# DeltaNet's output norm in two halves: the inner tokens inside the scan's last step, the outer ones behind it

## The chip, the cores and the metric

The kernel runs on one core of a Trainium2 chip. Its engines are TensorE (PE, with the weight loads shown apart as PEld), VectorE (DVE), ScalarE (ACT), GpSimd (POOL) and SyncE (SP, which issues most DMAs). The metric is the device time of one execution in microseconds. The kernel before takes 1773.67 us, the median of 3 runs (1772.34 to 1774.33).

## The reference, cut to what matters

One layer of a diffusion backbone works on 256 latent tokens and 256 context tokens, with 2048 channels. The combined input projection feeds latent attention and a bidirectional gated DeltaNet with 8 heads of 128 channels. The DeltaNet scans go over chunks of 64 tokens, one scan in each direction, the latent scans starting from the final context states; the outputs of both directions are added. What the change touches is the norm of that sum:

```
def dn_output(o, z, o_norm, dtype):
    y = rmsnorm(o.transpose(0, 2, 1, 3), o_norm) * silu(z)
    return y.reshape(b, t, h * dv)

merged = sigmoid(gate_mla) * (y_mla @ w_o_mla) + sigmoid(gate_dn) * (y_dn @ w_o_dn)
```

For each token and head, `o` is divided by the root mean square over its 128 channels, multiplied by a weight for each channel and by silu(z). Behind it stand the branch projections, the output projection, and a gated MLP with a convolution.

## The kernel before

Channels lie on the 128 partitions and tokens along the free dimension, so `o` is a tile of 128 partitions x 8 heads x 256 tokens, and `z` likewise. Every large product is made of a high and a low part of the float32 numbers: `split` writes the high part with ScalarE (L121) and the rest with VectorE (L122); `mm_hl` multiplies the high part of the weights with both parts of the activations (512 columns) and the low part of the weights with the high part alone (256 columns). Weights come over SP's queue in pieces of 512 KB and are split on the fly into six buffers of each part (NH = 6), each 512 columns wide.

A tile framework puts the other engines' instructions in an order by its own plan. TensorE's is written out by hand where `pe.pinned` is set, as it is during the scan and the norm. There a generator yields after each piece of scan work a number of nanoseconds, and a `Side` object fills that much time with other work: `fill` is the rest of the gate projections for the DeltaNet branch (16 tiles, four steps each, of which eight steps are done before) and the attention branch's projection with w_o_mla (16 tiles of two steps). A step is four pairs of products, counts as 1300, and `Side` makes steps while it owes time, so 56 + 32 = 88 steps in all. `ada` is the adaLN modulation, products on VectorE, with the share ADS = 0.3 of the time.

The scan has eight steps: the four chunks of the context, then the four latent ones; both directions are done at once, so at latent step `st` the forward scan writes chunk `st` and the backward scan chunk 3 - `st`. After the third latent step the tokens 64 to 191 (chunks 1 and 2) are complete; the last one adds to chunks 0 and 3. A step makes the products `kp` with the state, the subtraction `r` on VectorE, then yields CA = 4000; the products `yp`, copied to `y` by ScalarE, then CB = 3000; then the outputs `op`, the state's update `sp_` (not in the last step), the addition of `op` to `o` (L1355), and CC = 7000.

`o_norm` follows. It loads z's gate (`zo`) from memory, squares `o` by head on ScalarE (L1366, two buffers), sums the squares over the partitions with `col_sum` (four narrow products for each 128 tokens, against a column of ones), scales the sums (L1370), takes them to the power -0.5 on GpSimd in four quarters (`rsq`, L173), and multiplies `o` by `zo` head by head (L1374). After 5000 ns of fill it spreads each quarter of the factors over the partitions: `row_bcast` writes two diagonal matrices (the high and the low part, L179 to L185) and multiplies each with a matrix of ones, into `bp` (named obp in the profile); then `o` is multiplied by it (L1380) and split into `YD`, head by head, with ON = 3000 ns of fill for each quarter.

Then the pinned order ends, and the DeltaNet branch is projected: 16 tiles of w_o_dn, each eight pairs of products with `YD` (`brp<-YD` in the profile), then the output projection (`ops`).

`z` itself is made 440 us earlier, as the first eight tiles of another `fill`: `gate_fin` adds the two halves of the product, `z_fin` makes z (tanh(z/2) + 1) and multiplies by half of the norm's weight on ScalarE (L920); a DMA of ScalarE's queue stores it to `Zs`.

Of the kernel before, what the change touches and what calls it, by code (L numbers as in the profile page):

```python
# [8 lines left out]
F32 = mybir.dt.float32  # L9
F32R = mybir.dt.float32r  # L10
# [6 lines left out]
P = 128  # L17
D = 2048
KD = D // P
T = 256  # L20
# [11 lines left out]
AD = 0.55  # L32
GD0 = 2
SC = 7500
ON = 3000
CA = 4000
CB = 3000
CC = 7000
# [15 lines left out]
def hybrid_block(ctx: ExitStack, tc: tile.TileContext, io, dbg=None):  # L54
# [99 lines left out]
    def mm_hl(ps, M, w, x, first, last):  # L154

        hi, lo = w
        xf = x.rearrange("p a b -> p (a b)")
        if last and not first:
            pe.matmul(ps[:M, :T], lo, x[:, 0, :], start=False, stop=False)
            pe.matmul(ps[:M, :], hi, xf, start=False, stop=True)  # L160
        else:
            pe.matmul(ps[:M, :], hi, xf, start=first, stop=False)
            pe.matmul(ps[:M, :T], lo, x[:, 0, :], start=False, stop=last)
# [723 lines left out]
    Gs = dram.tile([2, P, KD, T], F32, name="Gs")  # L887
    pz = ctx.enter_context(pool_("pz", 3))

    def gate_fin(ps, out, fin):  # L890
        kept = isinstance(out, int)
        x = gk[:, out] if kept else pz.tile([P, T], F32, tag="zx", name="zx")
        gather(ps, P, x)
        if fin is None:
            act.activation(x, x, AF.Tanh, scale=0.5)
        else:
            fin(x)
        if not kept:
            act.dma_start(out, x)

    def gate_tiles(jobs):

        for w, f, out, fin in jobs:
            W = lazy_w(io[w][f])
            ps = psm.tile([P, 512], F32, tag="mm", name="gtp")
            for k in range(KD):
                mm_hl(ps, P, W(k * P), H[0][:, k], k == 0, k == KD - 1)
                if k % 4 == 3 and k < KD - 1:
                    yield 1300
            gate_fin(ps, out, fin)  # L910
            yield 1300
# [4 lines left out]
    def z_fin(x):  # L916
        t = pz.tile([P, T], F32, tag="zx", name="zt")
        act.activation(t, x, AF.Tanh, scale=0.5)
        dve.scalar_tensor_tensor(out=x, in0=t, scalar=1.0, in1=x, op0=ALU.add, op1=ALU.mult)
        act.activation(x, x, AF.Copy, scale=onh)  # L920

    fill = Side(gate_tiles([("wz", f, Zs[:, f], z_fin) for f in range(HEADS)] + [("wgm", f, Gs[0, :, f], None) for f in range(KD)]))
    pC = ctx.enter_context(ExitStack())
# [321 lines left out]
    def scan():  # L1245
# [11 lines left out]
        def load_kv(n):  # L1257
            kt, v = (jit[:, 2 * j + n % 2].rearrange("p (h c) -> p h c", c=P) for j in (0, 2))
            sync.dma_start(kt, KTs[steps[n]])
            sync.dma_start(v, Vs[steps[n]])  # L1260
            return kt, v
# [24 lines left out]
        for n, st in enumerate(steps):  # L1286
            kt, v = kv
            lat, first, last = st < 4, n == 0, n == 7
            if lat:
                qe = load_out(st)  # L1290
            if n and not last:
                ke = load_ke(n)
            if first:
                rs = [v[:, 4 * q : 4 * q + 4] for q in range(2)]
            else:
                rs = [ps1.tile([P, 4, P], F32, tag="r", name="r", bufs=2) for _ in range(2)]
                kps = [psa.tile([P, 4, P], F32, tag="aux", name="kp") for _ in range(2)]

                for h in range(HEADS):
                    for d in range(2):  # L1300
                        hs = slice(64 * d, 64 * d + 64)
                        pe.matmul(kps[h // 4][hs, h % 4], kt[:, h, hs], S[:, h, d ^ h % 2], start=True, stop=True)
                for h in range(HEADS):
                    dve.scalar_tensor_tensor(out=rs[h // 4][:, h % 4], in0=kps[h // 4][:, h % 4], scalar=negc[:, st, h : h + 1], in1=v[:, h], op0=ALU.mult, op1=ALU.add)
            if not last:
                kv = load_kv(n + 1)
            yield CA
            y = ps1.tile([P, 2, 4, P], F32, tag="y", name="y")
            yp = [psa.tile([P, 4, P], F32, tag="aux", name="yp") for _ in range(2)]
            for h in range(HEADS):  # L1310
                for d in range(2):
                    pe.matmul(yp[d][half_[d ^ h % 2], h // 2], tt[half_[d], h], rs[h // 4][half_[d], h % 4], start=True, stop=True)
            for d in range(2):
                act.copy(y[:, d], yp[d])
            if not last:
                tt = load_system(n + 1)
            yield CB
            if lat:
                op = [psm.tile([P, HEADS, 64], F32, tag="mm", name="op") for _ in range(2)]
                for h in range(HEADS):  # L1320
                    for m in half_:
                        for d in range(2):
                            r = d ^ h % 2
                            pe.matmul(op[r][m, h], y[half_[r], d, h // 2, m], av[half_[r], h], start=h == 0, stop=False)
                for h in range(HEADS):
                    for r in range(2):
                        for m in half_:
                            pe.matmul(op[r][m, h], S[:, h, r, m], qe[:, h, half_[r ^ h % 2]], start=False, stop=h == HEADS - 1)
            if not last and not first:
                for h in range(HEADS):  # L1330
                    for r in range(2):
                        act.activation(S[:, h, r], S[:, h, r], AF.Copy, scale=gend[:, r ^ h % 2, st, h : h + 1])
            if not last:
                for q in range(2):
                    h4 = slice(4 * q, 4 * q + 4)
                    sp = [psa.tile([P, 4, P], F32, tag="aux", name="sp_") for _ in range(2)]
                    for j in range(4):
                        h = 4 * q + j
                        for r in range(2):
                            pe.matmul(sp[r][:, j], ke[half_[r], h], y[half_[r], r ^ h % 2, h // 2], start=True, stop=True)  # L1340
                    for r in range(2):
                        if first:
                            act.copy(S[:, h4, r], sp[r])
                        else:
                            dve.tensor_tensor(out=S[:, h4, r], in0=sp[r], in1=S[:, h4, r], op=ALU.add)
            if lat:
                for d in range(2):
                    c = st if d == 0 else 3 - st
                    for e in range(2):
                        dst = o[:, e::2, 64 * c : 64 * c + 64]  # L1350
                        src = op[d ^ e][:, e::2] if d == 0 else op[d ^ e][:, e::2, ::-1]
                        if st < 2:
                            act.copy(dst, src)
                        else:
                            dve.tensor_tensor(out=dst, in0=src, in1=dst, op=ALU.add)  # L1355
            yield CC
        pS.close()

    def o_norm():

        zo = po.tile([P, HEADS, T], F32, name="zo")
        sync.dma_start(zo, Zs)
        osp = psa.tile([P, 16], F32, tag="aux", name="osp")
        for h in range(HEADS):
            sq = po.tile([P, T], F32, tag="osq", name="osq", bufs=2)
            act.activation(sq, o[:, h], AF.Square)  # L1366
            for t in range(2):
                col_sum(osp[:, 2 * h + t : 2 * h + t + 1], sq[:, t * P : (t + 1) * P], ones[:, 0:1])
        om = po.tile([P, 16], F32, name="om")
        dve.tensor_scalar(out=om, in0=osp, scalar1=1.0 / P, scalar2=EPS, op0=ALU.mult, op1=ALU.add)  # L1370
        for q in range(4):
            rsq(po, om[:, 4 * q : 4 * q + 4], om[:, 4 * q : 4 * q + 4], 4)
        for h in range(HEADS):
            dve.tensor_tensor(out=o[:, h], in0=zo[:, h], in1=o[:, h], op=ALU.mult)  # L1374
        yield 5000
        for q in range(4):
            bp = psa.tile([P, 512], F32, tag="aux", name="obp")
            row_bcast(po, bp, om[:, 4 * q : 4 * q + 4], 4)
            for h in (2 * q, 2 * q + 1):
                dve.tensor_tensor(out=o[:, h], in0=bp[:, (h % 2) * T : (h % 2) * T + T], in1=o[:, h], op=ALU.mult)  # L1380
                split(o[:, h], YD[:, h, 0], YD[:, h, 1])
            yield ON

    def e_fill():
        for f in range(KD):
# [6 lines left out]
    fill = Side(e_fill())  # L1392
    ada.bound = False
    pe.pinned = True
    for c in scan():
        fill(RE * c)
        ada(ADS * c)
    pM = ctx.enter_context(ExitStack())
    po = pM.enter_context(pool_("po", 1, "right"))
    YD = po.tile([P, HEADS, 2, T], F32R, name="YD")  # L1400
    for c in o_norm():
        fill(c)
    fill.finish()
    pe.pinned = False
    dump("o", o)
# [225 lines left out]
```

## Time and profile before

| what | value |
|---|---|
| median of the runs | 1773.67 us |
| profiled execution | 1780.3 us, span 1778.5 us |
| mean granted TensorE clock | 0.988 |
| busy share of PE, PEld, DVE, ACT | 98%, 84%, 76%, 53% |
| DMA | 415.59 MB, mean 234 GB/s |
| first and last column sum of the norm (`osp`) | 900.5 and 903.8 us |
| first and last broadcast (`obp`) | 907.1 and 919.0 us |
| first and last product with `YD` | 910.0 and 959.6 us |

A row of the profile's groups reads: line, engine, operation, output <- inputs, shape, count, busy time and mean duration, and behind the bar the idle time before them with what ended it. A timeline row begins with the start and the length in us. Matmuls overlap, so the length of one is more than the distance between two; a float32 product shows as two passes. Lines inside helpers stand for all their callers, so names of tiles tell them apart.

### The profile page before, as it was taken

The page shows a single profiled execution, that of the slowest core. Times are in us where ns is not written, and L with a number is a line of the kernel's source. Part 1 is how long each engine was busy: PE and PEld are TensorE (multiplying, and loading weights), DVE is VectorE, ACT ScalarE, POOL GpSimd, SP SyncE. Part 2 cuts the span into 40 slices and gives each one's busy share as a digit, 9 for nine tenths or more (in the row PEclk, how much of TensorE's full clock was granted, in tenths as well). Part 3 has the DMA queues.
Part 4 walks back from the last instruction along what each step waited for, and adds up shares of the span by engine and source line. Part 5 has one row for each costly group of instructions (what it writes and reads, how often), then busy time and mean ns, then how long its engine had stood idle before and what let it go on. Part 6 is the DMA issues. An engine that isn't in the chain of part 4 may idle for free.

```text
span 1778.5 us, 34182 instructions
## 1 busy us (share of the span) xinstructions
PE 1735.7 (98%) x12957; PEld 1502.4 (84%) x12957; DVE 1352.9 (76%) x2696; ACT 946.1 (53%) x1966; POOL 42.8 (2%) x49
## 2 busy tenths in 40 slices
PE   7999999999899998999989999999999999999999
PEld 5887887888788887887878888888888888888888
DVE  4787899879677877676779979888778888755554
ACT  3344554443667665665646556555555555544443
POOL 0000001000000000000010000000000000000000
PEclk9999999999999999999989999999999999999999
DMA  9982688773678768897947957777667776666662
GB/s 382 412 349 84 187 241 235 224 249 103 200 249 266 244 196 283 294 327 251 328 143 239 336 168 269 245 225 232 206 202 225 225 225 225 199 199 197 198 199 87
DMA packets 189397, 415.59 MB, mean 234 GB/s; under 512 B 56944, under 2 KB 95728, under 8 KB 186928
## 3 DMA queue, kind: packets, MB, share of 16 engines
q1 hardware_dynamic: 164064, 400.02, 69.0%
q10 hardware_dynamic: 25168, 13.39, 2.5%
q8 instruction: 102, 1.67, 0.4%
q14 instruction: 63, 0.52, 0.1%
HBM read 386.47 MB, written 26.74 MB: 232 GB/s over the span
## 4 chain that ended last, share of the span: by engine, by line
PE 53%; issue 19%; DVE 1%; DMA 1%; ACT 0%; POOL 0%; POOLq 0%; ACTq 0%; DVEq 0%; SPq 0%
PE fps L68 26%; PE dps L68 13%; PE gtp L68 6%; PE vps L68 1%; PE kps L68 1%; PE qps L68 1%; PE sps L68 1%; PE ivp L68 1%; PE yps L68 1%; DMA YM<-Ys 0%; DVE wlo L122 0%; PE ptp L68 0%; DMA Ys<-ryx 0%; PE kbp L68 0%; POOL om L173 0%
## 5 line engine op out<-in xcount | busy, mean ns | idle before, releaser
L122 DVE TENSOR_TENSOR wlo<-raw,whi 128x512 fp32r<-128x512 f32 (+1 forms) x940 | 634.9, 685 | 207.7 <-ACT whi L121 199.9
L121 ACT CAST whi<-raw 128x512 fp32r<-128x512 f32 (+1 forms) x940 | 575.1, 619 | 385.7 <-PE dps L68 113.7
L68 PE MATMUL fps<-H,whi 128*128 128x512 f32 x1376 | 474.7, 394 | 3.1 <-DVE H L1468 3.1
L68 PE MATMUL fps<-H,wlo 128*128 128x256 f32 x1376 | 372.2, 280 | 0.1
L68 PEld LDWEIGHTS fps<-H,whi 128*128 128x128 f32 x1376 | 253.5, 189 | 54.7 <-issue 1.9
L68 PEld LDWEIGHTS fps<-H,wlo 128*128 128x128 f32 x1376 | 259.6, 189 | 7.5 <-DVE wlo L122 0.5
L68 PE MATMUL gtp<-h,whi 128*128 128x512 f32 x640 | 234.3, 403 | 0.1
L68 PE MATMUL mmp<-h,whi 128*128 128x512 f32 x640 | 226.7, 397 | 0.0
L68 PE MATMUL dps<-GB,whi 128*128 128x512 f32 (+1 forms) x595 | 195.7, 378 | 0.0
L68 PE MATMUL gtp<-h,wlo 128*128 128x256 f32 x640 | 175.7, 285 | 2.7 <-DVE wlo L122 2.7
L68 PE MATMUL mmp<-h,wlo 128*128 128x256 f32 x640 | 175.9, 281 | 0.0
L68 PE MATMUL dps<-GB,wlo 128*128 128x256 f32 x560 | 154.1, 280 | 0.0
L68 PEld LDWEIGHTS gtp<-h,whi 128*128 128x128 f32 x640 | 122.0, 192 | 26.0 <-issue 1.0
L68 PEld LDWEIGHTS mmp<-h,whi 128*128 128x128 f32 x640 | 119.0, 188 | 24.4 <-ACT dkx L529 0.3
L68 PEld LDWEIGHTS gtp<-h,wlo 128*128 128x128 f32 x640 | 122.9, 192 | 8.6 <-DVE wlo L122 4.0
L68 PEld LDWEIGHTS dps<-GB,whi 128*128 128x128 f32 x595 | 109.2, 188 | 21.1
L68 PEld LDWEIGHTS mmp<-h,wlo 128*128 128x128 f32 x640 | 120.3, 188 | 3.0 <-issue 1.0
L279 DVE CUSTOM_DVE_ANT_0 rawa<-rawa,sch 128x1024 f32<-128x1024 f32 x71 | 86.6, 1220 | 27.4 <-DMA rawa<-in_wada 27.2
L68 PEld LDWEIGHTS dps<-GB,wlo 128*128 128x128 f32 x560 | 105.1, 188 | 0.6
L68 PE MATMUL fp<-h,gh 128*128 128x256 f32 (+1 forms) x448 | 84.8, 290 | 2.5 <-ACT h L68 1.7
L68 PEld LDWEIGHTS fp<-h,gh 128*128 128x128 f32 (+1 forms) x448 | 69.1, 188 | 7.6 <-issue 4.1
L68 DVE CUSTOM_DVE_ANT_0 rawa<-rawa,sch 128x1024 f32<-128x1024 f32 x57 | 69.2, 1215 | 0.0
(574 smaller groups left out, 2554.4 us busy)
## 6 DMA issues: line engine op xcount, KB each, us to landing
rawa<-in_wada SPq DMA_DIRECT2D x128, 512.0 KB, 4.9
raw<-in_wgate SPq DMA_DIRECT2D x82, 512.0 KB, 4.5
raw<-in_wval SPq DMA_DIRECT2D x82, 512.0 KB, 4.7
raw<-in_wdown SPq DMA_DIRECT2D x80, 512.0 KB, 4.1
wt<-in_wadas SPq DMA_DIRECT2D x16, 1024.0 KB, 11.2
raw<-in_wadab SPq DMA_DIRECT2D x32, 512.0 KB, 11.9
raw<-in_wgm SPq DMA_DIRECT2D x32, 512.0 KB, 5.2
raw<-in_wgd SPq DMA_DIRECT2D x32, 512.0 KB, 7.7
```

The source lines that it names most:

```text
L68: i = f(*a, **k)
L121: act.copy(hi, raw)
L122: dve.tensor_tensor(out=lo, in0=raw, in1=hi, op=ALU.subtract)
L279: (odve if ada.bound else dve).tensor_tensor_reduce(out=w, in0=w, in1=sch, scale=1.0, scalar=0.0, op0=ALU.mult, op1=ALU.add, accum_out=par ...
```

## The change

The norm is taken apart into two token ranges: INNER, tokens 64 to 191, and OUTER, the first and the last 64. The helpers `o_squares`, `o_sums`, `o_gate`, `o_scale` and `o_split` each take one of them. INNER's squares stand in the last scan step ahead of CA, its sums behind CA, its gate behind `yp`, its broadcasts and scaling behind CB and ahead of `op`. The last step yields no CC; behind its additions come OUTER's squares and gate, 2000 ns of fill, OUTER's sums, the end of the scan's pool, INNER's split into `YD`, 2600 ns of fill, and then for each half of the heads the broadcast, the scaling, the split and 1300 ns.

ScalarE and VectorE work on four heads x 128 tokens at a time (512 elements for each partition) instead of one head x 256. The gate is one instruction that multiplies z, the norm's weight and `o`, so the separate scaling of z (L920) goes. The broadcast is a plain float32 product of the factor, spread over 128 columns, with the identity, without high and low parts. `zo` is loaded in the last scan step, into rows 2 and 3 of the scan's buffer `jit`, whose last use was the step before. The store of each z tile is issued four pairs into the next tile instead of at once. The adaLN work is not offered any time once `YD` exists.

```diff
-ON = 3000
+ON = (2000, 2600, 1300)
...
         if not kept:
-            act.dma_start(out, x)
+            late.append(lambda: act.dma_start(out, x))
+            if fin is None:
+                late.pop()()
...
                 mm_hl(ps, P, W(k * P), H[0][:, k], k == 0, k == KD - 1)
+                if k == 3 and late:
+                    late.pop()()
...
-        act.activation(x, x, AF.Copy, scale=onh)
...
+            else:
+                sqs = o_squares(ps1, INNER)
             yield CA
+            if last:
+                zo = jit[:, 2:4].rearrange("p a (h t) -> p (a h) t", t=T)
+                sync.dma_start(zo, Zs)
+                om = o_sums(sqs)
...
+            else:
+                o_gate(zo, INNER)
             yield CB
+            if last:
+                for q in range(2):
+                    o_scale(om, q, INNER)
...
-            yield CC
+            if not last:
+                yield CC
+        sqs = o_squares(ps1, OUTER)
+        o_gate(zo, OUTER)
+        yield ON[0]
+        om = o_sums(sqs)
         pS.close()
-    def o_norm():
...
+        YD = pM.enter_context(pool_("po", 1, "right")).tile([P, HEADS, 2, T], F32R, name="YD")
+        merged.append(YD)
+        for q in range(2):
+            o_split(YD, q, INNER)
+        yield ON[1]
+        for q in range(2):
+            o_scale(om, q, OUTER)
+            o_split(YD, q, OUTER)
+            yield ON[2]
+
+    INNER, OUTER = slice(1, 3), slice(0, 4, 3)
+
+    def quarter(t, q, cs):
+        return t[:, 4 * q : 4 * q + 4].rearrange("p h (c i) -> p h c i", i=64)[:, :, cs]
+
+    def o_squares(pl, cs):
+        sqs = []
+        for q in range(2):
+            sqs.append(pl.tile([P, 4, 2, 64], F32, tag="osq", name="osq", bufs=2))
+            act.activation(sqs[q], quarter(o, q, cs), AF.Square)
+        return sqs
+
+    def o_sums(sqs):
+        osp = psa.tile([P, HEADS], F32, tag="aux", name="osp")
+        om = oms.pop()
+        for q in range(2):
+            for j in range(4):
+                h = 4 * q + j
+                col_sum(osp[:, h : h + 1], sqs[q][:, j].rearrange("p c i -> p (c i)"), ones[:, 0:1])
+        for q in range(2):
+            h4 = slice(4 * q, 4 * q + 4)
+            dve.tensor_scalar(out=om[:, h4], in0=osp[:, h4], scalar1=1.0 / P, scalar2=EPS, op0=ALU.mult, op1=ALU.add)
+            rsq(pd, om[:, h4], om[:, h4], 4)
+        return om
+
+    def o_gate(zo, cs):
+        for c in range(4)[cs]:
+            v, z = (t[:, :, 64 * c : 64 * c + 64] for t in (o, zo))
+            dve.scalar_tensor_tensor(out=v, in0=z, scalar=onh, in1=v, op0=ALU.mult, op1=ALU.mult)
+
+    def o_scale(om, q, cs):
+        bp = psa.tile([P, 4, P], F32, tag="aux", name="obp")
+        for j in range(4):
+            pe.matmul(bp[:, j], om[:, 4 * q + j : 4 * q + j + 1].broadcast_to([P, P]), ident, start=True, stop=True)
+        v = quarter(o, q, cs)
+        dve.tensor_tensor(out=v, in0=bp.rearrange("p h (c i) -> p h c i", i=64), in1=v, op=ALU.mult)
+
+    def o_split(YD, q, cs):
+        hi, lo = (quarter(YD[:, :, n], q, cs) for n in range(2))
+        v = quarter(o, q, cs)
+        act.copy(hi, v)
+        dve.tensor_tensor(out=lo, in0=v, in1=hi, op=ALU.subtract)
...
+    oms, merged = [pd.tile([P, HEADS], F32, name=f"om{n}") for n in range(2)], []
     for c in scan():
         fill(RE * c)
-        ada(ADS * c)
...
-    for c in o_norm():
-        fill(c)
+        if not merged:
+            ada(ADS * c)
+    YD, = merged
```

More of the change, by code (lines that the diff above doesn't have):

```diff
@@ L888, in hybrid_block @@
     pz = ctx.enter_context(pool_("pz", 3))
+    late = []
     def gate_fin(ps, out, fin):
@@ L1355, in scan @@
                             dve.tensor_tensor(out=dst, in0=src, in1=dst, op=ALU.add)
-            yield CC
-        pS.close()
-    def o_norm():
[L1361 to L1382, printed above, removed]
@@ L1394, in hybrid_block @@
     pe.pinned = True
+    pM = ctx.enter_context(ExitStack())
+    oms, merged = [pd.tile([P, HEADS], F32, name=f"om{n}") for n in range(2)], []
     for c in scan():
         fill(RE * c)
-        ada(ADS * c)
-    pM = ctx.enter_context(ExitStack())
-    po = pM.enter_context(pool_("po", 1, "right"))
-    YD = po.tile([P, HEADS, 2, T], F32R, name="YD")
-    for c in o_norm():
-        fill(c)
+        if not merged:
+            ada(ADS * c)
+    YD, = merged
     fill.finish()
```

## The prediction, made before the result was known

> **What bounds the kernel now.** The page's head and busy shares come first, then the windows around the end of the scan, which hold both pieces of code that the change touches.
>
> ```profile
> span 1778.5 us, 34182 instructions
> PE 1735.7 (98%) x12957; PEld 1502.4 (84%) x12957; DVE 1352.9 (76%) x2696; ACT 946.1 (53%) x1966; POOL 42.8 (2%) x49
> ...
> 900.00:907.00 7.00, 4.48 (x140) 3.17 (x138) 6.03 (x17) 3.72 (x10) 2.11 (x3) 0.88 0.54 155
> 907.00:910.00 3.00, 1.40 (x2) 0.57 (x2) 2.52 (x10) 0.78 (x2) 2.45 (x2) 0.50 0.00 0
> 910.00:915.00 5.00, 4.93 (x14) 3.88 (x14) 3.13 (x9) 0.50 (x3) 0.00 (x0) 0.50 0.33 95
> 925.00:960.00 35.00, 35.00 (x201) 30.44 (x200) 34.60 (x82) 23.49 (x53) 0.00 (x0) 1.00 0.61 186
> ...
> 905.00:905.50 0.50, 0.50 (x4) 0.27 (x2) 0.14 (x1) 0.00 (x0) 0.50 (x1) 0.85 0.80 328
> 905.50:915.25 9.75, 6.59 (x17) 4.45 (x16) 6.83 (x20) 2.42 (x6) 3.95 (x4) 0.50 0.22 71
> ```
>
> Columns of the windows: length, then busy time of PE, PEld, DVE, ACT and POOL, the granted clock, the DMA share, GB/s. TensorE is busy nearly everywhere, so what TensorE loses the kernel loses. From 900 to 915 it loses: o_norm stands there, its fill work has run out, and from 905.5 to 915.25 the granted clock is 0.50. DMA is almost idle from 907 to 910, so loads are not the cause. The timeline of PE names the holes.
>
> ```profile
> 900.53 0.43 PE L68 MATMUL osp<-ones,osq 128*32 128x1 f32 x32
> 901.56 0.61 PE L68 MATMUL osp<-ones,osq 128*32 128x1 f32 x32 [0.59 <-ACT osq L1366]
> ...
> 903.91 0.50 PE L68 MATMUL brp<-YM,whi 128*128 128x512 f32 x1
> ...
> 907.07 1.40 PE L68 MATMUL obp<-rb_d,onesr 128*128 128x512 f32 x2 [1.40 <-DVE rb_d L185]
> 910.07 0.77 PE L68 MATMUL brp<-YD,whi 128*128 128x512 f32 x1 [1.61 <-DVE rb_l L180]
> ...
> 915.55 0.50 PE L68 MATMUL obp<-rb_d,onesr 128*128 128x512 f32 x1 [0.45 <-DVE rb_d L185]
> ...
> 917.05 0.39 PE L68 MATMUL obp<-rb_d,onesr 128*128 128x512 f32 x1
> 917.28 0.39 PE L68 MATMUL brp<-YD,whi 128*128 128x512 f32 x1
> ...
> 959.83 0.40 PE L68 MATMUL ops<-MA,whi 128*128 128x512 f32 x1
> ```
>
> **What the hole costs.** The four groups of column sums run from 900.53 to 903.91, 3.38 us, where four times the first group's 0.43 is 1.72: 1.66 lost waiting for squares. Idle time before obp 1.40, before the first product with YD 1.61, at 915.55 another 0.45. At clock 0.50 two stretches of work take twice their time: obp from 907.07 (1.40, so 0.70 lost) and 910.07 to 915.10 (5.03, so 2.5 lost). Together 8.3 us.
>
> **What goes and what comes on VectorE.**
>
> ```profile
> L185 DVE TENSOR_TENSOR rb_d<-ident,rb_h 128x512 fp32r<-128x512 f32 x4 | 2.7, 684 | 0.0
> L185 DVE TENSOR_TENSOR rb_d<-ident,rb_l 128x512 fp32r<-128x512 f32 x4 | 2.7, 682 | 0.0
> L1380 DVE TENSOR_TENSOR o<-obp,o 128x256 f32<-128x256 f32 x8 | 3.1, 416 | 2.3 <-PE obp L68 2.3
> ...
> 865.98 1.29 DVE L122 TENSOR_TENSOR wlo<-raw,whi 128x512 fp32r<-128x512 f32 x2 [0.32 <-PE op L68]
> 868.73 1.41 DVE L1355 TENSOR_TENSOR o<-op,o 128x256 f32<-128x256 f32 x4
> ```
>
> Back to back, four instructions of 256 elements take 1.41 us, two of 512 take 1.29: 0.34 and 0.60 for each further one. The diagonals go (2.7 + 2.7, and eight 128x4 instructions), and 24 instructions of 256 (gate, scale, split; 8.1 us) become 12 of 512 (7.2). VectorE is relieved of some 6.5 us, and the path from the norm to a broadcast loses two 0.68 us instructions per quarter. On ScalarE eight squares and eight casts become four and four of twice the width; costed at nothing, since it sits idle more than half of the tail (3.72 of 7, 0.50 of 5).
>
> **The broadcasts get dearer on TensorE.** Before, eight 128x512 products at 0.23 (917.05 to 917.28) are 1.84 us. After, 16 plain float32 products against the identity. The same form stands in the first microseconds:
>
> ```profile
> 15.66 1.16 PE L68 MATMUL scp<-ident,sc 128*128 128x128 f32 x8
> 16.75 1.06 PE L68 MATMUL pss<-sq,ones 128*32 128x512 f32 x8
> ...
> L68 PE MATMUL brp<-YD,whi x100: 389/393/397, 924.7 to 959.6; 128*128 128x512 f32 x100
> ...
> 878.61 1.97 PE L68 MATMUL kp<-S,jit 128*64 128x128 f32 x32
> ...
> 888.88 1.16 PE L68 MATMUL op<-av,y 64*64 64x64 f32 x64
> ...
> 891.99 0.50 PE L68 MATMUL gtp<-h,whi 128*128 128x512 f32 x1
> ```
>
> Four products are eight recorded passes, 1.09 us from start to start, so 16 cost 4.36: 2.5 us more. Were each pass as cheap as one of kp (1.97/32 = 0.06), 16 would cost 1.97 and the loss would be 0.1; 128x128 weights are what scp has, so I take 2.5. The column sums keep their number (2 x 8 x 4 against 8 x 2 x 4).
>
> **The new order, laid out.** One fill step is four pairs of a weight tile; 100 pairs in 34.9 us give 0.352 a pair, 1.41 a step. The scan used to pay 112000 ns of fill and o_norm the rest; now the scan with its tail pays 98000 + 7000 + 7200 = 112200. At 1300 a step that puts 3 steps behind kp, 2 behind yp, 2 behind op (ON[0]), 2 behind the outer sums (ON[1]), 1 behind each broadcast and 1 at the end: the 88 steps now reach to the end instead of being spent at 905.7. Starting where kp ends (880.5): fill 884.7, inner sums 885.6, yp 886.6, fill 889.4, two inner broadcasts 891.6, op (888.88 to 891.99, so 3.1) 894.7, fill 897.5, outer sums 898.4, fill 901.2, broadcast 902.3, fill 903.7, broadcast 904.8, fill 907.6. Then 128 pairs with YD at 0.352 end at 952.7, where the old ones end at 959.83: 7.1 us earlier, with nothing waiting. The pieces above give 8.3 - 2.5 = 5.8. I take 6.2, nearer to the pieces, since some wait will remain.
>
> **What hides the norm's chain.**
>
> ```profile
> 904.64 0.17 DVE L1370 TENSOR_SCALAR om<-osp 128x16 f32<-128x16 f32 x1
> 904.89 4.56 POOL L173 TENSOR_TENSOR om<-om,half 128x4 f32<-128x4 f32 x4 [194.44 <-DVE om L1370]
> 906.04 0.17 DVE L179 CAST rb_h<-om 128x4 fp32r<-128x4 f32 x1 [0.90 <-POOL om L173]
> ```
>
> From the last sums (903.91) to the first om (906.04) it is 2.1 us, each further quarter about 1.1 (4.56/4); ON[1] covers 2.8 and the second broadcast has 2.5 more, so neither waits. Uncovered it would cost up to 2.1. Behind op stand four adds (1.41) and two squares of about 0.6 against 2.8 of fill: even; a VectorE queue with two splits ahead would add 1.3. Behind the last broadcast scale, cast and subtract (about 2) stand against 2.8 of fill. VectorE has some 14 us of work for the 13 us from 894.7 to 907.6, carried by the six split buffers (six steps, 8.5 us) filled before. YD takes the scan pool's place and waits for its last readers, of which the outer gate is one; it is off by 899, when the inner split is wanted.
>
> **The z tiles, 440 us earlier.** Dropping the scaling of z by the norm's weight frees ScalarE of eight instructions, and the store moves behind four pairs of the next tile.
>
> ```profile
> 462.78 0.42 ACT L918 ACTIVATE zt<-zx 128x256 f32<-128x256 f32 x1
> 463.91 0.51 ACT L920 ACTIVATE zx<-zx,onh 128x256 f32<-128x256 f32 x1 [0.71 <-DVE zx L919]
> 464.44 0.33 ACTq L899 DMA_DIRECT2D Zs<-zx  x1
> 464.82 0.60 ACT L1013 ACTIVATE ksq<-kps 128x512 f32<-128x512 f32 x1 [0.40 <-ACT zx L920]
> ...
> 465.47 0.43 PE L68 MATMUL ks<-ones,ksq 128*32 128x1 f32 x32 [2.19 <-ACT ksq L1013]
> ```
>
> Here TensorE stands 2.19 us for a square queued behind that scaling and its wait for VectorE. Straight behind zt (463.2) the square comes 1.6 earlier; if the store's trigger takes the scaling's place and waits as long, 0.5; a reordered stage could make it nothing. I take 0.8. The other seven end no TensorE wait.
>
> **The load of zo** moves from the tail into the last step and into the freed rows of jit.
>
> ```profile
> 869.88 0.27 PE L68 MATMUL sp__10804<-y,jit 64*128 64x128 f32 x1
> ...
> 875.84 13.40 SPq L127 DMA_DIRECT2D raw<-in_wodn  x7
> 892.10 0.33 SPq L1362 DMA_DIRECT2D zo<-Zs  x1
> ...
> 898.75 0.43 DVE L1374 TENSOR_TENSOR o<-zo,o 128x256 f32<-128x256 f32 x1 [1.45 <-DMA zo<-Zs]
> ```
>
> It lands 6.6 us after issue. Its rows of jit are last read by the state products of the step before, which end at 870.1, so SP can issue it ahead of the seven w_o_dn loads; the inner gate wants it near 886. A megabyte among those loads costs no TensorE time as long as the split buffers are full.
>
> **Sum.** -6.2 - 0.8 = -7.0 us. The profiled execution took 1780.3 (span 1778.5 and 1.8 around it), so 1773.3 there; it lies 6.6 above the median 1773.67, and the same difference gives **1766.7**. The scan's tail also pays 1500 ns less to the adaLN work, which moves one product on VectorE to a later stage; it weighs nothing there unless the third rival holds.
>
> **The clock, by row and by rule.** The clock fell at 905.25 to 905.5, when the longest idle time before it was 0.59 us, behind 3.4 us of column sums; a thin stretch was enough. The Trainium skill (TensorE: Matmul & The Clock Gate, "What's actually happening") has it fall after an idle window of about 3.4 us; the trace does not agree, and by that rule the new order, which has no such gap, keeps full speed with the sum as it stands.
>
> **Rivals.**
> - *Half the gain is eaten by queue order on VectorE* (16%): splits ahead of the adds, the sums or om delay TensorE twice by about 1.5 us. For it: 34.60 of 35 busy behind the hole. Against: 6.5 us less to do. 1766.7 + 3 = 1769.7.
> - *The clock falls anyway* (8%): the outer sums and broadcasts are a thin stretch too. 10 us at half clock lose 5: 1771.7. Against: the sums now come in 0.86 us between dense steps.
> - *The gain is given back behind it* (6%): the branch stage is short of VectorE, not TensorE, and starting it earlier only makes it wait. About 1773.5. Against: TensorE is 35.00 of 35 busy there.
> - *zo comes late* (6%, the other side): SP keeps the seven loads ahead, zo lands at 898.7 as now, the inner gate stands in VectorE's queue from 886 and blocks splits, scales and op's adds behind it. TensorE's buffered splits end near 894.5, adds, squares and sums follow 898.7 by 5: 7 us of stall, and 5 more by the clock. -7 + 12 = +5: 1778.7. It decides from an issue later than about 885.
>
> **The numbers.** The forecast has 64%, its own range 1763.5 to 1769.5. Low end: 9.0 (laid out and cheap passes together, 7.1 + 2.4 less 0.5 of waits) and 1.6 for z: 1763.0. High end holds the second rival: 1772.0; the last two stay out. About 0.2% (3.5 us) can be told from no change: faster 64 and three quarters of the first rival's 16, 76%; same 4 + 8 + 5 = 17%; slower 7%.
>
> **What would show it.** Right: no osp or broadcast row with an idle time over 0.5, clock 1.00 from 895 to 925, first product with YD near 907.6 and the first with MA near 952.7, broadcasts of 1.09 per four, ks at 465 with under 1.7 idle, SP's zo before 885. Wrong: 0.50 in a window of the tail, a gate waiting for zo, or the wout stage no earlier than 957.

## The result, and the profile after

The changed kernel takes 1771.57 us in the median of 20 runs, the kernel before 1774.72 in 20 runs taken beside it. These medians lie 3.15 us apart; the ratio estimated from the runs is 0.9971, with a 95% interval of 0.9961 to 0.9982, and that is 5.1 us less (3.2 to 6.9), a small gain that is clear of the noise. 7.0 were forecast. The profiled execution has a span of 1770.7 us, 7.8 less than the one before; a part of that lies in stages that no term of the forecast names, as the balance further down shows. Three executions among the runs of the experiments (one each of no_cover, own_bufs and the kernel before) ran at a mean granted clock of 0.56 to 0.76 and stand in no ratio.

The first view is the timeline of PE through the changed tail: start, length, what ran, and in brackets the idle time ahead of it, of which there is none. The second is the windows answering to those shown of before (length, busy time of PE, PEld, DVE, ACT and POOL, granted clock, DMA share, GB/s).

```profile
875.52 1.97 PE L68 MATMUL kp<-S,jit 128*64 128x128 f32 x32
881.79 0.71 PE L68 MATMUL osp<-ones,osq 128*32 128x1 f32 x64
882.49 1.33 PE L68 MATMUL yp<-r,tt 64*64 64x128 f32 x32
886.62 1.95 PE L68 MATMUL obp<-ident,om 128*128 128x128 f32 x16
888.50 1.16 PE L68 MATMUL op<-av,y 64*64 64x64 f32 x64
...
894.60 0.71 PE L68 MATMUL osp<-ones,osq 128*32 128x1 f32 x64
898.13 1.05 PE L68 MATMUL obp<-ident,om 128*128 128x128 f32 x8
898.95 0.48 PE L68 MATMUL brp<-YM,whi 128*128 128x512 f32 x1
900.41 1.05 PE L68 MATMUL obp<-ident,om 128*128 128x128 f32 x8
904.09 0.39 PE L68 MATMUL brp<-YD,whi 128*128 128x512 f32 x1
...
948.62 0.39 PE L68 MATMUL ops<-MA,whi 128*128 128x512 f32 x1
```

```profile
900.00:907.00 7.00, 7.00 (x45) 6.28 (x44) 6.65 (x13) 4.13 (x8) 0.00 (x0) 1.00 0.64 194
907.00:910.00 3.00, 3.00 (x19) 2.61 (x18) 2.74 (x7) 2.07 (x5) 0.00 (x0) 1.00 0.50 182
910.00:915.00 5.00, 5.00 (x32) 4.41 (x31) 4.88 (x12) 3.38 (x8) 0.00 (x0) 1.00 0.65 206
```

The hole is gone: TensorE is busy throughout and the clock stays at 1.00. The first product with MA starts at 948.62 instead of 959.83, 11.2 us earlier, of which 3.1 stood already at the last kp, where the tail begins.

Then something is given back. In the view of a tile's instructions (count, then ns, then first and last start) the output projection `ops` runs from its first to its last product:

```profile
L68 PE MATMUL kp<-S,jit x224: 272/273/323, 738.1 to 877.2; 128*64 128x128 f32 x112
L68 PE MATMUL ops<-MA,whi x136: 277/392/397, 948.6 to 1039.0; 128*128 128x512 f32 x120, 128*128 128x256 f32 x16
L68 PE MATMUL ops<-MB,wlo x128: 277/280/395, 951.6 to 1042.0; 128*128 128x256 f32 x128
```

The same rows of before:

```profile
L68 PE MATMUL kp<-S,jit x224: 272/273/323, 740.1 to 880.3; 128*64 128x128 f32 x112
L68 PE MATMUL ops<-MA,whi x136: 282/391/398, 959.8 to 1045.9; 128*128 128x512 f32 x120, 128*128 128x256 f32 x16
L68 PE MATMUL ops<-MB,wlo x128: 277/282/282, 962.8 to 1048.8; 128*128 128x256 f32 x128
```

So the tail, from the last kp to the first ops, takes 948.6 - 877.2 = 71.4 us instead of 79.5, and the output projection 93.4 instead of 89.0: 8.1 gained, 4.4 lost. TensorE's waits in that stage were none before; after the change the waits of the stage read (who waited for whom, total us, times, longest):

```profile
DVE rawa L279 <- DMA rawa<-in_wada: 14.4, 12, 2.8
...
PEld ops L68 <- DVE wlo L122: 4.5, 4, 1.8
...
PE ops L68 <- DVE wlo L122: 3.3, 3, 1.5
```

`wlo` is the low part of a split weight, written by VectorE. TensorE's weight loads wait 4.5 us for such parts, as much as the stage lost; its products wait 3.3, since some of that time still passes under the product ahead.

The waits of SP's queue, which issues the loads, read:

```profile
SPq L260 <- DVE parts L279: 18.2, 7, 3.2
```

An adaLN load (rawa) takes one of the eight buffers that it shares with the weights. After the change such a load was issued again and again only when the adaLN product just ahead had ended, so it seems to have been given that product's buffer; before, such loads waited 1.5 us in all for products, and nearly always a further load was out when a product began. One such turn, on SP, on VectorE and on TensorE:

```profile
995.50 0.33 SPq L260 DMA_DIRECT2D rawa<-in_wada  x1
```

```profile
994.24 1.22 DVE L279 CUSTOM_DVE_ANT_0 rawa<-rawa,sch 128x1024 f32<-128x1024 f32 x1 [0.91 <-DMA rawa<-in_wada]
...
1000.92 1.22 DVE L279 CUSTOM_DVE_ANT_0 rawa<-rawa,sch 128x1024 f32<-128x1024 f32 x1 [2.79 <-DMA rawa<-in_wada]
```

```profile
1003.14 0.40 PE L68 MATMUL ops<-MB,wlo 128*128 128x256 f32 x1 [1.33 <-DVE wlo L122]
```

The product ends at 995.5, only then the next load is issued; it lands 5.4 us later, VectorE stands 2.79 us for it with splits of weights queued behind, and TensorE misses one of these for 1.33.

The stage was short of neither VectorE nor the memory. The windows of the whole stage, before and then after:

```profile
959.80:1048.80 89.00, 89.00 (x528) 78.94 (x527) 79.64 (x153) 49.82 (x97) 0.00 (x0) 1.00 0.85 292
```

```profile
948.60:1042.00 93.40, 90.10 (x529) 78.84 (x527) 76.92 (x148) 47.31 (x97) 0.00 (x0) 1.00 0.80 266
```

Before, VectorE did more work there (79.64 us) and the DMAs moved more (292 GB/s) without one wait of TensorE.

### The profile page after: what moved, and what is told of

It reads as the page before. It is cut to its first block, busy times and chain, and to the rows that moved or that the text cites. A ratio compares the mean times of both kernels' runs of the same rounds, so it can differ in the third digit from the quotient of the medians.

```text
span 1770.7 us, 34206 instructions
## 1 busy us (share of the span) xinstructions
PE 1729.0 (98%) x12981; PEld 1499.6 (85%) x12981; DVE 1350.2 (76%) x2671; ACT 941.5 (53%) x1950; POOL 43.5 (2%) x49
## 4 chain that ended last, share of the span: by engine, by line
PE 63%; issue 8%; DVE 2%; ACT 1%; DMA 1%; POOL 0%; POOLq 0%; ACTq 0%; DVEq 0%; SPq 0%
PE fps L68 26%; PE dps L68 13%; PE gtp L68 11%; PE brp L68 2%; PE vps L68 1%; PE kps L68 1%; PE sps L68 1%; PE qps L68 1%; PE ivp L68 1%; PE yps L68 1%; PE op L68 1%; PE kp L68 1%; DVE wlo L122 0%; PE yp L68 0%; DMA tt<-Xq 0%
## 5 line engine op out<-in xcount | busy, mean ns | idle before, releaser
L122 DVE TENSOR_TENSOR wlo<-raw,whi 128x512 fp32r<-128x512 f32 (+1 forms) x940 | 634.2, 685 | 206.2 <-ACT whi L121 199.9
L68 PE MATMUL gtp<-h,whi 128*128 128x512 f32 x640 | 230.2, 397 | 0.1
## 6 DMA issues: line engine op xcount, KB each, us to landing
raw<-in_wadab SPq DMA_DIRECT2D x32, 512.0 KB, 11.9
```

What stands on the lines that cost most here:

```text
L68: i = f(*a, **k)
L122: dve.tensor_tensor(out=lo, in0=raw, in1=hi, op=ALU.subtract)
```

## The experiments

Two theories stood at the start. One: missing fill made the hole. The other: VectorE's chain of diagonals and narrow instructions made it. For the loss behind it: late adaLN loads, or a stage short of VectorE or memory anyway. Stage lengths below come from one profiled execution of each kernel by the rows shown above; the ratio is to the kernel before on the same chip. "rawa" is VectorE's wait for adaLN loads in the output projection, "wlo" the wait of TensorE's weight loads there for the low parts.

| kernel | tail, us | output projection, us | rawa, us | wlo, us | first gtp to first ks, us | ratio and interval |
|---|---|---|---|---|---|---|
| before | 79.5 | 89.0 | 3.1 | 0 | 38.8 | 1 |
| after | 71.4 | 93.4 | 14.4 | 4.5 | 34.0 | 0.9971 (0.9961 to 0.9982) |
| z_only | 78.9 | 89.0 | 8.9 | 0 | 33.9 | 0.9997 (0.9982 to 1.0012) |
| fill_only | 76.5 | 91.6 | 11.9 | 2.7 | 34.5 | 0.9990 (0.9973 to 1.0006) |
| plain_only | 75.1 | 89.4 | 8.3 | 0 | 38.5 | 0.9987 (0.9974 to 1.0000) |
| plain_fill | 75.3 | 93.7 | 13.8 | 2.9 | 36.8 | 0.9999 (0.9980 to 1.0018) |
| sq6 | 72.0 | 91.7 | 12.4 | 2.2 | 38.6 | 0.9992 (0.9974 to 1.0010) |
| diag | 80.6 | 94.2 | 15.7 | 5.4 | 38.2 | 1.0012 (0.9997 to 1.0026) |
| no_cover, no_cover_b | 75.9 | 89.1 | 8.8 | 0 | 38.9 | 0.9991 (0.9977 to 1.0004) |
| ada_always | 71.4 | 92.0 | 12.8 | 3.0 | 34.2 | 0.9967 (0.9951 to 0.9984) |
| ahead3 | 71.4 | 90.9 | 12.2 | 2.1 | 37.5 | 1.0022 (1.0005 to 1.0039) |
| own_bufs | 71.4 | 89.2 | 6.8 | 0 | 34.9 | 0.9958 (0.9942 to 0.9974) |

What an output projection has over 89 us is its wlo column within 0.5, but for plain_fill: 4.7 against 2.9, at a clock of 0.98 where all others have 1.00. Most intervals include 1; of the changed kernels only after, ada_always and own_bufs are shown to be faster than before. Tail, output projection and the 0.5 us of the z part add up to a change inside the timed interval for most; for sq6 and diag it lies 0.2 and 1.2 us outside, for ahead3 7.6 outside.

**The z part alone.**

```diff
 (before)
-            act.dma_start(out, x)
+            late.append(lambda: act.dma_start(out, x))
...
+                if k == 3 and late:
+                    late.pop()()
...
-        act.activation(x, x, AF.Copy, scale=onh)
...
-            dve.tensor_tensor(out=o[:, h], in0=zo[:, h], in1=o[:, h], op=ALU.mult)
+            dve.scalar_tensor_tensor(out=o[:, h], in0=zo[:, h], scalar=onh, in1=o[:, h], op0=ALU.mult, op1=ALU.mult)
```

> The kernel before with the z part alone: no scaling of z by the norm's weight on ScalarE, the store four pairs into the next tile, the weight multiplied in by the gate of the old o_norm. Forecast's theory: only the wait of ks for ksq gets shorter (2.19 to about 1.65 us), 0.5 to 0.8 us in all, the tail from the last kp to the first product with MA stays at 79.5 us. Rival: the z part carries a good share of the gain, as the stretch from the first gtp to the first ks (38.8 us before, 34.0 after) suggests: 2 to 4 us, and that stretch near 34.

The tail is near that of before (78.9 against 79.5), the time the same. What the z part does is in two views of the changed kernel, ScalarE and then PE:

```profile
462.88 0.42 ACT L924 ACTIVATE zt<-zx 128x256 f32<-128x256 f32 x1
464.00 0.33 ACTq L901 DMA_DIRECT2D Zs<-zx  x1
464.38 0.60 ACT L1018 ACTIVATE ksq<-kps 128x512 f32<-128x512 f32 x1 [1.08 <-DVE zx L925]
```

```profile
465.03 0.43 PE L68 MATMUL ks<-ones,ksq 128*32 128x1 f32 x32 [1.65 <-ACT ksq L1018]
```

The store's trigger stands where the scaling stood and waits for VectorE just as long, so 2.19 became 1.65: 0.54 us, in all seven kernels with the z part (1.65) against all five without (2.19). The stretch of 34 or 38 us is not the z part: fill_only, without it, has 34.5, ahead3, with it, 37.5. It goes with the clock granted between 432 and 460: 0.76 to 0.82 in the six kernels with 37.5 to 38.9 us, 0.88 in plain_fill, 0.94 in own_bufs, 1.00 in the four with 33.9 to 34.5.

**Fill alone, plain broadcasts alone, and both.**

```diff
 (before: fill_only)
-ON = 3000
+ON = 1300
-            yield CC
+            yield CC if st != 3 else 2000
-        yield 5000
+        yield 2600
 (before: plain_only; plain_fill has both)
-            row_bcast(po, bp, om[:, 4 * q : 4 * q + 4], 4)
+            for j in range(4):
+                pe.matmul(bp[:, j * P : j * P + P], om[:, 4 * q + j : 4 * q + j + 1].broadcast_to([P, P]), ident, start=True, stop=True)
```

> The kernel before with its fill work spread over the norm as in the change (the last step's CC 2000, then 2600 and four times 1300), and the old norm otherwise. Theory A, the hole is missing fill: the tail from the last kp to the first product with MA falls from 79.5 us to 73 to 75, the clock stays at 1.00, 4 to 6 us gained. Theory B, the hole is VectorE's chain of diagonals and narrow instructions: the tail stays at 78 to 79.5, the waits for rb_d and o only move, and the time does not change by over 1.5 us.

> The kernel before with plain float32 broadcasts in the old norm, nothing else. Theory now: VectorE's order is the longer half of the hole, since in the changed kernel with diagonals TensorE waited for them even under fill; the tail from the last kp to the first product with MA falls from 79.5 to 75 to 77 us, though TensorE's broadcasts take 2.2 us more and no fill is left behind 905. Rival: without fill the shorter chain stays uncovered and the clock falls as before: 78 to 80 us.

> The kernel before with plain float32 broadcasts and the fill spread over the norm, but the norm whole behind the scan, head by head, and z as before. Theory: the halves add little to these two; alone they took 4.4 and 3.0 us off the tail, together 7 to 7.5, so the tail is 72 to 72.5 us against 71.4, and the time lies with the changed kernel's if the output projection loses as much to late adaLN loads (91 to 93 us), 3 to 4 us below it if not (89). Rival: the column sums wait for the two buffers of squares as before (1.2 to 1.7 us) and the clock falls behind them, so the halves are worth 3 us or more: tail 74 us or more.

Fill alone takes 3.0 us off the tail, plain broadcasts alone 4.4, both together 4.2. In fill_only TensorE still waits 1.9 us for diagonals with fill on both sides, so neither theory's range (73 to 75, 78 to 79.5) was met and both held a part. In the other two these waits are gone, and what is left is the column sums, then the clock. In plain_fill, PE and then the windows:

```profile
893.74 0.43 PE L68 MATMUL osp<-ones,osq 128*32 128x1 f32 x32
894.84 0.61 PE L68 MATMUL osp<-ones,osq 128*32 128x1 f32 x32 [0.67 <-ACT osq L1366]
895.75 0.61 PE L68 MATMUL osp<-ones,osq 128*32 128x1 f32 x32 [0.29 <-ACT osq L1366]
896.65 0.61 PE L68 MATMUL osp<-ones,osq 128*32 128x1 f32 x32 [0.29 <-ACT osq L1366]
```

```profile
897.00:898.00 1.00, 1.00 (x21) 0.90 (x22) 0.61 (x2) 0.00 (x0) 0.00 (x0) 1.00 0.98 377
898.00:899.00 1.00, 1.00 (x6) 0.94 (x5) 1.00 (x5) 0.00 (x0) 0.35 (x1) 0.59 0.25 86
899.00:900.00 1.00, 1.00 (x4) 0.81 (x3) 1.00 (x4) 0.67 (x2) 1.00 (x2) 0.50 0.07 27
900.00:901.00 1.00, 1.00 (x4) 0.80 (x4) 1.00 (x3) 0.22 (x1) 1.00 (x2) 0.50 0.00 0
901.00:902.00 1.00, 1.00 (x8) 0.90 (x7) 0.52 (x2) 0.32 (x1) 1.00 (x1) 0.70 0.00 0
```

The expectation of plain_fill, that the halves add little, was wrong: they are worth 3.9 us there (75.3 against 71.4). The next kernel asks why.

**Six buffers for the squares.**

```diff
 (plain_fill)
-            sq = po.tile([P, T], F32, tag="osq", name="osq", bufs=2)
+            sq = po.tile([P, T], F32, tag="osq", name="osq", bufs=6)
```

> plain_fill (old norm behind the scan, plain broadcasts, spread fill) with six buffers for the squares instead of two. Theory: what the halves are still worth there (tail 75.3 us against 71.4) is the column sums' waiting for squares (1.3 us) and the half clock that follows this thin stretch; with the squares ready the sums run in 1.7 us, the clock stays at 1.00 and the tail is 72 to 73 us. Rival: 1.7 us of one-column products drop the clock by themselves, or the squares come no earlier because ScalarE does them in the same order: 74 to 75.5 us.

All sums now run without a gap, and the clock stays at 1.00 behind them:

```profile
898.03 1.90 PE L68 MATMUL osp<-ones,osq 128*32 128x1 f32 x128
```

```profile
895.00:900.00 5.00, 5.00 (x150) 4.11 (x146) 1.84 (x5) 3.68 (x12) 0.00 (x0) 1.00 0.78 277
900.00:905.00 5.00, 5.00 (x32) 4.52 (x33) 4.98 (x15) 2.53 (x6) 4.40 (x4) 1.00 0.49 164
```

The tail is 72.0 us, so without halves and without wide instructions all but 0.6 of the 8.1 us is there. Plain broadcasts, fill behind the sums, and squares ready for the sums are what closes the hole; the halves are one way to the third. That sq6 is faster than before as a whole is not shown: its output projection loses 2.7 us, and the interval of its ratio includes 1.

**The changed kernel with diagonals.**

```diff
 (after, in o_scale)
-            pe.matmul(bp[:, j], om[:, 4 * q + j : 4 * q + j + 1].broadcast_to([P, P]), ident, start=True, stop=True)
...
+        dve.tensor_copy(rh, r)
+        dve.tensor_tensor(out=rl, in0=r, in1=rh, op=ALU.subtract)
...
+        for v, dg in zip((rh, rl), dgs):
+            dve.tensor_tensor(out=dg, in0=idb, in1=v.unsqueeze(2).broadcast_to([P, 4, P]), op=ALU.mult)
+        row_spread(bp.rearrange("p a b -> p (a b)"), dgs, 4)
```

> The changed kernel with the broadcasts by diagonals (a high and a low part, written by VectorE) instead of plain float32 products. Theory A: with the chain covered by fill the diagonals lie beside TensorE's work, and TensorE saves 2.2 us (eight products at 0.23 against 4.05): tail 69 to 71.4 us against 71.4, the time equal or up to 2 us less. Theory B: the diagonals are what makes the chain too long: waits of TensorE for rb_d of 2 us and more in the tail, tail 74 or more, the time 3 us up.

The tail is 80.6 us, longer than before the change. VectorE between the first om and the first broadcast, and then PE:

```profile
890.85 0.17 DVE L1426 CAST rb_h<-om 128x4 fp32r<-128x4 f32 x1 [0.90 <-POOL om L173]
890.93 1.22 DVE L279 CUSTOM_DVE_ANT_0 rawa<-rawa,sch 128x1024 f32<-128x1024 f32 x1
...
892.08 0.16 DVE L1427 TENSOR_TENSOR rb_l<-om,rb_h 128x4 f32<-128x4 f32 x1
892.15 0.68 DVE L1430 TENSOR_TENSOR jit<-ident,rb_h 128x512 fp32r<-128x512 f32 x1
892.75 0.68 DVE L1430 TENSOR_TENSOR jit<-ident,rb_l 128x512 fp32r<-128x512 f32 x1
```

```profile
892.98 1.30 PE L68 MATMUL obp<-jit,onesr 128*128 128x512 f32 x2 [2.54 <-DVE jit L1430]
```

An adaLN product of 1.22 us sits between the two parts of one factor. In the pinned order this wait stands ahead of op, and 2.54 us of it end uncovered; there is a second one of 1.90 in the outer half, and the clock falls twice. With the halves the tail is longer than before when each broadcast needs four VectorE instructions in a row.

**No fill between the steps.**

```diff
 (after; the same kernel twice)
-ON = (2000, 2600, 1300)
+ON = (7200, 0, 0)
```

> The changed kernel with all 7200 ns of the tail's fill ahead of the outer sums, none between sums, broadcasts and splits. By the prediction's covers: 2.1 us of waiting for om, about 1 for the second om less the first broadcast, about 2 for scale, cast and subtract less the last fill step, so 3 to 4.5 us, and the clock likely at 0.50 for up to 10 us, another 2 to 5: tail 75 to 80 us against 71.4. Rival: wide instructions and plain broadcasts alone close the hole and the fill's place is of no account: under 73 us.

> The kernel without fill between sums, broadcasts and splits once more, for its trace at an undisturbed clock. Tail 75 to 80 us against 71.4 by the prediction's covers (om 2.1, second om about 1, scale, cast and subtract about 2, and the clock); under 73 us if the fill's place is of no account. The timed ratio to the kernel before, 0.9991 against 0.9971 for the changed kernel, speaks for 3.5 us.

The trace is that of no_cover_b, the ratio that of no_cover. The tail is 75.9 us, 4.5 more than with fill. One wait shows:

```profile
905.75 2.66 PE L68 MATMUL obp<-ident,om 128*128 128x128 f32 x16 [2.37 <-POOL om L173]
```

It is the om chain, put at 2.1; the clock is 0.72 from 905 to 910 behind it. The other waits did not come.

**The adaLN loads.**

```diff
 (after: ada_always)
-        if not merged:
-            ada(ADS * c)
+        ada(ADS * c)
 (after: ahead3)
-        half, ahead = None, [load(0), load(1)]
+        half, ahead = None, [load(0), load(1), load(2)]
...
-            if i < 126:
-                ahead.append(load(i + 2))
+            if i < 125:
+                ahead.append(load(i + 3))
 (after: own_bufs)
-            w = wr.tile([P, GR], F32, tag="raw", name="rawa", bufs=NR)
+            if ada.own and 86 <= i < 96:
+                w = ada.own[0].tile([P, GR], F32, tag="rawo", name="rawa", bufs=3)
+            else:
+                w = wr.tile([P, GR], F32, tag="raw", name="rawa", bufs=NR)
...
         merged.append(YD)
+        ada.own.append(pM.enter_context(pool_("pow", 1, "right")))
```

> The changed kernel with the adaLN work offered its 0.3 share of the whole tail again, as before the change (one product more ahead of the output projection). If leaving that out is what made the adaLN loads late in the output projection, the stage returns to 89 to 90 us and the time falls 3 us; if it is the planner dealing out buffers anew, the stage stays at 91 to 94 us with SP waiting over 10 us for products, and the tail grows by 0 to 1 us for the product put into it.

> The changed kernel with the adaLN weights loaded three products ahead instead of two. Theory: the output projection (first to last product 89.0 us before, 93.4 after) was held up by adaLN loads that SP issues only when the product before has freed their buffer, so with one more ahead it takes 89 to 90 us, the waits of VectorE for rawa in it fall from 14.4 to under 5 us, and the kernel gains 3 to 4 us on the changed one. Rival: VectorE has too much to do there since the stage starts earlier; then the stage stays at 93 and the time does not move.

> The changed kernel with three buffers of their own, in the room that the scan left, for the adaLN weights of products 86 to 95, which fall in the output projection. Theory: SP issued those loads only when the product before had freed the buffer that the load was to take (18.2 us of SP's waits on the products against 1.5 before the change), VectorE stood for them and the splits behind it came late; with other buffers the loads go early, VectorE's waits for rawa fall under 5 us, the output projection takes 89 to 90 us instead of 93.4, the time falls 3 to 4 us below the changed kernel. Rival: the memory or VectorE itself is short there; then 92 to 94 us stay whatever the buffer.

With buffers of their own the output projection takes 89.2 us, TensorE waits for no split in it, and SP's waits for a product fall from 18.2 to 2.2:

```profile
SPq L263 <- DVE parts L282: 2.2, 1, 2.2
```

```profile
L68 PE MATMUL ops<-MA,whi x136: 277/392/397, 947.9 to 1034.1; 128*128 128x512 f32 x120, 128*128 128x256 f32 x16
L68 PE MATMUL ops<-MB,wlo x128: 277/280/384, 950.9 to 1037.1; 128*128 128x256 f32 x128
```

VectorE still waits 6.8 us for rawa, over the 5 expected, and no weight load waits for it: over all twelve kernels the stage stays at 89.0 to 89.4 us up to 8.9 us of such waiting and is 90.9 or more from 11.9 on. SP's waiting alone does not decide: no_cover_b has 15.1 us of it and a stage of 89.1. Nor is own_bufs the plan of before again, since only 12 adaLN products fall into its stage instead of 15 after and 17 before; that fewer products alone are not the cure is seen from before, which lost nothing with 17. The ratio of 0.9958 (7.5 us; 4.6 to 10.3) is the lowest here; its interval overlaps that of the changed kernel, so the clear evidence for the 4.2 us between them is the stage. Offering adaLN work again (ada_always) leaves 92.0 and 18.4 us of SP's waits: leaving it out was not the cause. One more load ahead (ahead3) shortens the stage by 2.5 to 90.9 where 89 to 90 was expected, SP's waits stay (19.3), and the kernel is slower than before (1.0022, 3.9 us) instead of faster. Its scan is 2.3 us longer than before (142.5 against 140.2 from first to last kp); that the third load takes a buffer from the weights there is a guess. With a tail 8.1 us shorter than before, 2.3 in the scan are far from explaining 3.9 us more, and the rest is open.

## Why the prediction was right, and where it was not

**The hole.** 6.2 us were taken, 8.1 measured. The mechanism was right, as the experiments show cause by cause: squares, diagonals and missing fill made the waits, and the clock fell behind them. The layout of 7.1 was nearly right; the discount for remaining waits was not, since none remained. Two prices were also lower than taken: the eight inner broadcast products (16 recorded passes) cost 1.88 us (886.62 to 888.50) and the four of each outer half some 0.82 (898.13 to the next product at 898.95), 3.5 in all instead of 4.36, and the 32 column sums of one range (64 passes) 0.71 instead of 0.86. The first product with YD came 26.9 us behind the last kp, against 27.3 laid out.

**Covers.** The om chain at 2.1 us was right (2.37 when bared). The queue on VectorE, the first rival, did not stretch it. The inner gate did wait for zo, 1.32 us, but it began at 875.47, more than ten us before its product was scaled (888.01), since SP issued the load ahead of the seven w_o_dn loads as forecast:

```profile
867.12 0.33 SPq L1317 DMA_DIRECT2D jit<-Zs  x1
...
873.01 14.40 SPq L127 DMA_DIRECT2D raw<-in_wodn  x7
```

**The z part.** Taken 0.8, between 0.5 and 1.6; measured 0.54, and by the way named for the low end, the trigger in the scaling's place.

**The clock.** It stayed at 1.00, so the second rival fell, for the reason given against it: dense sums. sq6 and plain_fill show that the sums alone do not drop it; stretched by gaps from 1.90 to 3.5 us they did. Whether the gaps count or the length of the thin stretch is not separated.

**What failed.** The sum ended with the hole: the sentence that the adaLN work "weighs nothing there unless the third rival holds" put the stage behind at nothing, and it cost 4.4 us. The third rival, with 6%, had it that gain is given back behind the tail, but with the wrong stage and mechanism: not a branch stage short of VectorE (that one ran dense) but loads issued late in the output projection, so that VectorE stood and split too late. Leaving out adaLN work in the tail was not the cause (ada_always). That the planner deals out buffers anew for the rest of the program when a few instructions move is the likeliest reading of the new order of loads, and no run shows the planner's choice itself. Seven of the eleven changed kernels in the table lost 1.9 us or more there; own_bufs shows that it can be taken back.

**The balance.** -8.1 + 4.4 - 0.5 = -4.2 us, within the measured 3.2 to 6.9. The profiled pair differs by 7.8: the other 3.6 are 2.6 between the first ks and the last kp and 1.0 behind the output projection, which no term of the forecast names. The stretch with the falling clock does not enter: the first gtp came 4.3 later and the stretch from it to ks was 4.8 shorter, 0.5 together, as much as the z part.

**The number.** 1766.7 was forecast. The measured 1771.57 lies outside the forecast's own range of 1763.5 to 1769.5. It lies inside the whole range only because the high end, 1772.0, had room for a clock that falls, which did not happen; the room was filled by a loss in a place that the sum did not have. So far the number was luck. The 1.9 us that the hole gave beyond what was taken hid a part of the 4.4.

## What to carry to other kernels

A hole on the bounding engine can be several causes in a row, and taking one away alone shows the next: fill, the length of the chain and the two buffers of squares each hid behind the other. Where a broadcast or a norm stands in a hand-written order, the number of in-order instructions between a result and the engine that waits for it can weigh more than the cost of the matmul that replaces them: here plain broadcasts alone shortened the tail by 4.4 us though they cost TensorE more (3.5 us in the changed kernel against 1.84). When a planner places loads, look at the stages behind the edit for loads that wait for the work they are to feed, and give them buffers of their own.

## What the runs showed of the hardware

In plain_fill the granted clock fell behind column sums with gaps of 0.67, 0.29 and 0.29 us, and in sq6 it did not fall behind the same sums run in 1.90 us. In plain_fill the half-speed stretch lasts 3.4 us, worked out from the clocks of its windows (0.82 of the microsecond from 898, two whole ones, 0.6 of the one from 901). The Trainium skill (TensorE: Matmul & The Clock Gate, "What's actually happening") gives a free-running window of about 3.4 us, which agrees with that length; its condition of an idle window does not agree, since no idle time here was over 0.67 us.

In the five kernels whose source is that of before around 432 to 460 us (before, fill_only, plain_only, plain_fill, sq6) the clock there was 0.82, 1.00, 0.82, 0.88 and 0.82, and the stretch from gtp to ks took 38.8, 34.5, 38.5, 36.8 and 38.6 us: some 4 us, nearly as much as the whole change. With one profiled execution of each, chance and plan are not told apart. Executions of one and the same kernel do differ: of the 35 of the kernel before beside the first experiments, the three shortest (1769.6 to 1770.3 us) had a mean granted clock of 0.995, the three longest (1780.1 to 1780.6) one of 0.988 to 0.990.

In the changed kernel a gate with three operands over 512 elements (L1418) took 0.75 us, a two-operand instruction of that width (L1425, L122) 0.68.
